# LRU gelu and convolution as side tasks, one weight buffer fewer, and a reordered routing and closing

## The chip, the cores and the metric

One core of one Trainium2 chip runs the whole program. The metric is the device time in microseconds. Before the change three timed runs gave 3310.49, 3309.92 and 3304.97 us, median 3309.92. The profiled execution is a further one, of 3298.6 us.

## The reference, cut to what matters

One layer of a hybrid backbone on 1024 latent tokens and 256 context tokens of width 1024, all in float32.

- An adaLN-modulated RMSNorm of the tokens goes through one input projection. Its columns feed three mixers; of the context, only what the latent scans start from is needed.
- The LRU mixer, which the change touches, has 8 blocks of 128 channels. For each block: a convolution of 4 taps along the tokens (context and latent apart) gives `u`; for each of two directions `r = sigmoid(u @ wa + ba)`, `i = sigmoid(u @ wi + bi)`, `log_a = -8 r softplus(-lambda)`, `v = sqrt(1 - exp(2 log_a)) i u`, and a scan `h = a h + v` that runs through the context and then the latent tokens. The branch is `(h_forward + h_backward) * gelu(y)`, with `y` from another 128 columns of the projection.
- The other two mixers (gated DeltaNet, Mamba-2 SSD) are not touched. The three branches are projected, gated, summed and projected again (`w_out`), and added to the input.
- A second modulated norm feeds a mixture of 32 experts in 4 groups: group logits and expert logits from a router matrix, the best group by its softmax, the two best experts in it by theirs. Each expert computes `(silu(x w1) * (x w3)) w2` on the tokens routed to it, the two results of a token are weighted and added to the residual, and a last RMSNorm gives the output.

## The kernel before, in words

Every large product is split into three fp32r matmuls: an operand is cast to a rounded part (`hi`, ScalarE) and the rest (`lo`, VectorE or GpSimd), and hi·hi, hi·lo and lo·hi are summed in PSUM.

**Phase 1** runs a list of jobs. A job (`run`, L351) takes one block of 128 projection columns: it fetches the split weights (`WBlocks.get`), and multiplies them with the latent tokens (16 groups of 3 matmuls of 512 columns, into one of two PSUM tiles `pj` of 1024 columns), with the context (24 matmuls of 256 columns, into a bank `pjc`), or with both. Then `done` hands the PSUM tile to side tasks. These are generators in a list; between the matmuls of a job `tick` (L392) steps each one that is due. What is due is decided when the program is written out, by a model of the engines' clocks (`Clock`); on the chip each engine then works through its instructions in that fixed order. `live` counts the `pj` tiles that are in use: with two in use the next latent job is not written out before a side task has given one back (`give`). `until(flags)` steps the side tasks, and writes no further job, until the flags are set.

In the LRU stage the jobs of block b are LX+b (latent and context, its values go to the convolution), two jobs of the other mixers that need the context alone, LY+b (latent, its values go to the gelu), and two more such context jobs; four latent jobs for the merge gates follow the last block. `lru_jobs` (L707) makes them. After LX+b, `done` waits with `until` for block b-2 to be written to memory, loads the gate weights `lw` and adds the side task `lru_conv` (L626). That task runs the convolution on one tile `u` of 1280 columns (context and latent), adds one `lru_scan` (L651) for each direction, waits for both, adds their results and multiplies with the gelu. `lru_scan` makes two gates by matmuls on `u` (`psg`, three pieces of up to 512 columns) and a Tanh, and then the decay (`th`, `ea`), the input and the scan; its tiles `tr`, `th` and `ea` have one buffer for each direction, and block b starts its gates when block b-1 has read them for the last time but for `ea` (flag `lt`). After LY+b, `gelu` waits with `until` for block b-1 to be written to memory, since there is one gelu buffer `gl`.

`WBlocks` keeps raw and split weights. The split of the next block goes into the slot that the last job has left. There are two slots for split weights and one for raw ones, and during this stage one more of each (`extra`, in the pool `wx`).

**Out projection and routing.** `out_proj` (L1854) takes eight tiles T of 128 tokens: 48 matmuls each, then `router` of tile T-1 (transposes, logits in `lg`), and `post` of tile T (residual, norm, `h`). After the loop come `route_tokens(0, 7)`, the router of tile 7 and `route_tokens(7, 8)`, which turn logits into experts on VectorE. `route` then counts the tokens of each expert and builds a table of token indices by 16 small matmuls of one-hot matrices `R` and `Bt`.

**Experts.** `experts` (L2256) streams 32 experts: weights are split on ScalarE and VectorE (`wh`, `wl`, three buffers), rows of tokens are gathered, transposed and split (`take`), and the results are scattered to memory (`ys`) by indirect DMAs on GpSimd's queue. `load_x2` loads the residual, two tiles of tokens at a time, on the same queue. After a loop over overflow blocks, `combine` (L2302) loads both results of each token, weights and adds them, and applies the last norm, one tile of 128 tokens after the other.

Of the kernel before, what the change touches and what calls it, by code (L numbers as in the profile page):

```python
# [34 lines left out]
MERGE = (0, 2, 1)  # L35
RAWS = 7
# [232 lines left out]
class Core:  # L269
# [356 lines left out]
    def lru_conv(self, b, ps, wts):  # L626

        lp = self.lp
        u = lp.tile([P, CTX + SEQ], F32, tag="u", name="u")
        cw, cb = self.pp["lcw"][:, 4 * b:4 * b + 4], self.pp["lcb"][:, b:b + 1]  # L630
        yield from self.conv(u[:, CTX:], ps[True], cw, cb, SEQ)
        self.give(ps[True])
        yield from self.wait(("lx", b))
        yield from self.conv(u[:, 0:CTX], ps[False][:, :CTX], cw, cb, CTX)
        self.give(ps[False])
        hs = [None, None]
        for d in range(2):
# [3 lines left out]
        o = u[:, CTX:]  # L641
# [9 lines left out]
    def lru_scan(self, b, d, u, wts, hs):  # L651
# [5 lines left out]
        def gate(w, tag):  # L657
            o = lp.tile([P, n], F32, tag=tag, name="gate", bufs=1)
            i = 4 * b + 2 * d + w
            for n0 in (0, 512, 1024):  # L660
                yield from self.room()
                n1 = min(n, n0 + 512)
                pg = self.aux.tile([P, 512], F32, tag="aux", name="psg")
                nc.tensor.matmul(pg[:, :n1 - n0], lhsT=wts[:, 2 * d + w, :], rhs=u[:, n0:n1], start=True, stop=True)
# [10 lines left out]
        th = lp.tile([P, n], F32, tag=f"th{d}", name="th", bufs=1)  # L675
        ea = lp.tile([P, n], F32, tag=f"ea{d}", name="ea", bufs=1)
# [11 lines left out]
        nc.vector.scalar_tensor_tensor(out=ti, in0=ti, scalar=1.0, in1=u, op0=ALU.add, op1=ALU.mult)  # L688
# [18 lines left out]
    def lru_jobs(self):  # L707
        jobs = []
        for b in range(KT):
            ps = {}  # L710

            def gelu(_, p, lat, b=b, ps=ps):
                if b:
                    self.until(("lre", b - 1))
                ps["ge"] = g = self.lp.tile([P, SEQ], F32, tag="gl", name="gl", bufs=1)
# [4 lines left out]
            def done(_, p, lat, b=b, ps=ps):  # L720
                ps[lat] = p
                if not lat:
                    self.flags.add(("lx", b))
                else:
                    if b > 1:
                        self.until(("lre", b - 2))
                    w = self.lp.tile([P, 4, P], F32, tag="lw", name="lw")
                    self.nc.sync.dma_start(out=w, in_=self.io["lw"][b])
                    self.add(self.lru_conv(b, ps, w))
# [1124 lines left out]
    def out_proj(self, acc):  # L1854
# [20 lines left out]
        def post(T, ps):  # L1875
# [4 lines left out]
            nc.vector.tensor_tensor(out=x2, in0=x2, in1=xt, op=ALU.add)  # L1880
            h = mg.tile([P, D], F32, tag="gt", name="h2", bufs=2)
# [788 lines left out]
```

## Time and profile before

| | us |
|---|---|
| timed runs, median of 3 | 3309.92 |
| profiled execution | 3298.6 |
| its span, first to last instruction | 3296.9 |
| PE busy (89%) | 2918.7 |
| VectorE busy (65%) | 2144.6 |
| ScalarE busy (48%) | 1569.8 |
| GpSimd busy (23%) | 756.0 |
| mean granted TensorE clock | 0.954 of full speed |

PE is the engine that multiplies matrices, DVE is VectorE, ACT is ScalarE, POOL is GpSimd and SP is the engine that issues most DMAs. All times are us from the span's start unless a row says otherwise. A row of a timeline is: start, length, engine, line, operation, tile written <- tiles read, shape, count; in brackets the idle time ahead of it and what ended that. Rows of the same kind that follow each other are merged into one, with a count. Every instruction passes through a helper of the clock model, so all carry the line L255; tiles tell them apart. A matmul of 512 columns whose operands are plain float32, as for `psg`, counts as two.

### The profile page before, as it was taken

The numbers are of one execution on the slowest core, as the hardware profiler recorded it, in microseconds if no ns is written. First come the engines' busy times: TensorE is split into PE (matmuls) and PEld (weight loads), VectorE is DVE, ScalarE is ACT, GpSimd is POOL, SyncE is SP. The second block draws the span as 40 slices with busy tenths as digits, with TensorE's granted clock in tenths as the row PEclk, the third lists the DMA queues.
The fourth block names the chain that finished last, engine by engine and source line by source line (L and its number), as shares of the span: only waits on it lengthen the run. The fifth ranks groups of instructions, "written<-read, shape, count | busy, mean of one in ns | idle before, by whom it ended". The sixth has DMA issues, their size and how long they took to land. (4 is left out here: it accounts for less than half of the span.)

```text
span 3296.9 us, 47286 instructions
## 1 busy us (share of the span) xinstructions
PE 2918.7 (89%) x18539; PEld 2331.5 (71%) x18539; DVE 2144.6 (65%) x3734; ACT 1569.8 (48%) x2260; POOL 756.0 (23%) x638
## 2 busy tenths in 40 slices
PE   7878789989999889899999997979786899999992
PEld 3756667777768667677888886757565788878882
DVE  4676766744744744878888873226635878787785
ACT  4556565344315415455555544111112667677674
POOL 1112121202612621111121111121000233333333
PEclk9989999989999999999999999989898899999996
DMA  5112122211111102021111122455445688898896
GB/s 193 58 58 85 63 76 72 97 40 52 40 38 64 45 26 75 28 52 36 42 37 47 47 78 84 148 216 186 166 158 209 246 331 319 296 342 302 309 351 229
DMA packets 125313, 439.95 MB, mean 133 GB/s; under 512 B 18456, under 2 KB 44312, under 8 KB 99488
## 3 DMA queue, kind: packets, MB, share of 16 engines
q1 hardware_dynamic: 77712, 363.84, 30.7%
q10 hardware_dynamic: 35920, 52.07, 5.2%
q0 software_dynamic: 11456, 21.00, 1.8%
q8 instruction: 147, 2.41, 0.3%
q14 instruction: 78, 0.64, 0.1%
HBM read 393.76 MB, written 64.05 MB: 139 GB/s over the span
## 5 line engine op out<-in xcount | busy, mean ns | idle before, releaser
L255 PE MATMUL pj<-hhi,whi 128*128 128x512 f32 x1616 | 680.4, 422 | 16.9 <-ACT hhi L255 6.8
L255 PE MATMUL pj<-hhi,wlo 128*128 128x512 f32 x1616 | 640.2, 397 | 6.9 <-POOL wlo L255 3.7
L255 PE MATMUL pj<-hlo,whi 128*128 128x512 f32 x1616 | 640.5, 397 | 6.5 <-DVE hlo L255 4.8
L255 DVE TENSOR_TENSOR wl<-raw,wh 128x2048 fp32r<-128x2048 f32 x188 | 448.0, 2403 | 102.7 <-ACT wh L255 100.4
L255 POOL TENSOR_TENSOR wlo<-raw,whi 128x1024 fp32r<-128x1024 f32 x75 | 190.2, 2536 | 1011.4 <-ACT whi L255 939.9
L255 ACT ACTIVATE wh<-raw 128x2048 fp32r<-128x2048 f32 x188 | 360.8, 1919 | 128.2 <-PE psu L255 102.3
L255 PEld LDWEIGHTS pj<-hhi,whi 128*128 128x128 f32 x1616 | 306.1, 190 | 82.6 <-issue 8.4
L255 PEld LDWEIGHTS pj<-hhi,wlo 128*128 128x128 f32 x1616 | 304.8, 189 | 83.3 <-POOL wlo L255 5.3
L255 PEld LDWEIGHTS pj<-hlo,whi 128*128 128x128 f32 x1616 | 306.2, 190 | 72.1 <-DVE hlo L255 7.0
L255 ACT ACTIVATE whi<-raw 128x1024 fp32r<-128x1024 f32 x145 | 152.9, 1057 | 358.1 <-PE pj L255 268.2
L255 PE MATMUL psu<-wl,xh 128*128 128x512 f32 x576 | 227.2, 394 | 3.0 <-DVE wl L255 3.0
L255 PE MATMUL psu<-wh,xh 128*128 128x512 f32 x576 | 227.9, 396 | 0.0
L255 DVE TENSOR_TENSOR wlo<-raw,whi 128x1024 fp32r<-128x1024 f32 x70 | 91.6, 1309 | 208.8 <-ACT whi L255 208.0
L255 PE MATMUL psu<-wh,xl 128*128 128x512 f32 x576 | 226.1, 392 | 0.9 <-DVE xl L255 0.9
L255 ACT ACT_TABLE_LOAD x124 | 159.1, 1283 | 81.2 <-DVE xt L255 32.3
L255 POOL TENSOR_TENSOR yo<-yo,m 128x1024 f32<-128x1024 f32 x35 | 103.6, 2960 | 183.3 <-ACT yo L255 183.2
L255 PE MATMUL psg<-u,lw 128*128 128x512 f32 (+1 forms) x192 | 88.7, 598 | 55.8 <-issue 52.9
L255 PEld LDWEIGHTS psu<-wl,xh 128*128 128x128 f32 x576 | 108.8, 189 | 29.9 <-DVE wl L255 8.4
L255 PEld LDWEIGHTS psu<-wh,xl 128*128 128x128 f32 x576 | 108.7, 189 | 23.6 <-DVE xl L255 1.7
L255 PEld LDWEIGHTS psu<-wh,xh 128*128 128x128 f32 x576 | 109.2, 190 | 22.2 <-ACT xh L255 0.2
L255 PE MATMUL psy<-wh,xh 128*128 128x512 f32 x288 | 117.5, 408 | 0.7 <-ACT xh L255 0.7
L255 PE MATMUL psy<-wh,xl 128*128 128x512 f32 x288 | 114.6, 398 | 0.2 <-DVE xl L255 0.2
(474 smaller groups left out, 5959.2 us busy)
## 6 DMA issues: line engine op xcount, KB each, us to landing
raw<-in_w SPq DMA_DIRECT2D x188, 1024.0 KB
raw<-in_w_in SPq DMA_DIRECT2D x119, 512.0 KB
wr<-in_w_mod ACTq DMA_DIRECT2D x32, 512.0 KB
gate<-gt ACTq DMA_DIRECT2D x48, 256.0 KB
st<-br SPq DMA_DIRECT2D x24, 512.0 KB
raw<-in_w_branch SPq DMA_DIRECT2D x24, 512.0 KB
gt<-gate SPq DMA_DIRECT2D x24, 512.0 KB
wm<-in_w_mod SPq DMA_DIRECT2D x8, 1024.0 KB
```

The source lines that it names most:

```text
L255: return f(*args, **kw)
```

## The change

- `gelu` becomes a side task (`gated`) that keeps its PSUM tile until block b-2 is written to memory and `gl`, now with two buffers, is free. The job list no longer stops there.
- The wait for block b-2 and the load of `lw` move from `done` into `lru_conv`.
- `u` becomes `ul` (latent, 1024 columns) and `uc` (context, 256). The scans are added when the latent part is convolved; the gates take the two latent pieces first and wait for the context part (flag `lc`) before the third. The product with `u` becomes two instructions.
- In `lru_scan` a wait for the sum of block b-1 (flag `lru`) stands ahead of `ea`.
- `WBlocks.extra` no longer adds a third slot for split weights; the second raw slot stays.
- `out_proj`: behind the matmuls of T = 7 come `route_tokens(0, 6)` and the residual of tile 7, then the router of tile 6 and the rest of `post`; at the end the router of tile 7 and `route_tokens(6, 8)`. The Exp of the group logits moves to `route_weights`.
- `route`: `R` and `Bt` are built four at a time by three VectorE instructions with broadcast operands; GpSimd has no part in it.
- `experts`: one weight split instead of two stands ahead of the first tokens; `load_x2` is issued at experts 20, 23, 26 and 29 instead of 29 to 32.
- `combine`: two VectorE instructions add both weighted results to the residual, in place of a ScalarE scaling, a VectorE instruction and a GpSimd addition.

```diff
-    def lru_conv(self, b, ps, wts):
+    def lru_conv(self, b, ps):
         lp = self.lp
-        u = lp.tile([P, CTX + SEQ], F32, tag="u", name="u")
+        if b > 1:
+            yield from self.wait(("lre", b - 2))
+        wts = lp.tile([P, 4, P], F32, tag="lw", name="lw")
+        self.nc.sync.dma_start(out=wts, in_=self.io["lw"][b])
+        ul = lp.tile([P, SEQ], F32, tag="ul", name="ul")
+        uc = lp.tile([P, CTX], F32, tag="uc", name="uc")
-        yield from self.conv(u[:, CTX:], ps[True], cw, cb, SEQ)
+        yield from self.conv(ul, ps[True], cw, cb, SEQ)
         self.give(ps[True])
-        yield from self.wait(("lx", b))
-        yield from self.conv(u[:, 0:CTX], ps[False][:, :CTX], cw, cb, CTX)
-        self.give(ps[False])
         hs = [None, None]
         for d in range(2):
-            self.add(self.lru_scan(b, d, u, wts, hs))
+            self.add(self.lru_scan(b, d, uc, ul, wts, hs))
+        yield from self.wait(("lx", b))
+        yield from self.conv(uc, ps[False][:, :CTX], cw, cb, CTX)
+        self.give(ps[False])
+        yield
+        self.flags.add(("lc", b))
...
-            for n0 in (0, 512, 1024):
+            for n0, n1 in ((CTX, CTX + 512), (CTX + 512, n), (0, CTX)):
+                if not n0:
+                    yield from self.wait(("lc", b))
...
+        if b:
+            yield from self.wait(("lru", b - 1))
         ea = lp.tile([P, n], F32, tag=f"ea{d}", name="ea", bufs=1)
...
             def gelu(_, p, lat, b=b, ps=ps):
-                if b:
-                    self.until(("lre", b - 1))
-                ps["ge"] = g = self.lp.tile([P, SEQ], F32, tag="gl", name="gl", bufs=1)
+                self.add(gated(b, p, ps))
+
+            def gated(b, p, ps):
+                if b > 1:
+                    yield from self.wait(("lre", b - 2))
+                ps["ge"] = g = self.lp.tile([P, SEQ], F32, tag="gl", name="gl")
...
+            if T == 7:
+                self.route_tokens(0, 6)
+                x2 = resid(T, ps)
             if prev:
                 router(*prev)
-            prev = post(T, ps)
-        self.route_tokens(0, 7)
+            prev = post(T, x2 if T == 7 else resid(T, ps))
         router(*prev)
-        self.route_tokens(7, 8)
+        self.route_tokens(6, 8)
...
-        for n in range(16):
...
+        for a in range(0, 16, 4):
+            R = rp.tile([P, 4, P], F32, tag="R", name="R", bufs=2)
+            v.tensor_tensor(out=R, ...is_equal)
+            Bt = rp.tile([P, 4, NC], F32, tag="Bt", name="Bt", bufs=2)
+            v.tensor_tensor(out=Bt, ...is_equal)
+            v.tensor_tensor(out=Bt, in0=Bt, in1=tok..., op=ALU.mult)
...
-        st.split(2)
+        st.split(1)
         x = take(0)
-        st.split(WB - 2)
+        st.split(WB - 1)
...
-            if e > NE - 4:
-                self.load_x2(2 * (e - NE + 3))
+            if e in X2:
+                self.load_x2(2 * X2.index(e))
...
         def weigh(T):
-            nc.scalar.activation(out=y[T][:, 0, :], in_=y[T][:, 0, :], func=AF.Copy, scale=self.wt[:, 0, T:T + 1])
-            nc.vector.scalar_tensor_tensor(out=y[T][:, 0, :], in0=y[T][:, 1, :], scalar=self.wt[:, 1, T:T + 1],
-                                           in1=y[T][:, 0, :], op0=ALU.mult, op1=ALU.add)
+            x2 = self.x2[:, T, :]
+            for k in range(2):
+                nc.vector.scalar_tensor_tensor(out=x2, in0=y[T][:, k, :], scalar=self.wt[:, k, T:T + 1], in1=x2,
+                                               op0=ALU.mult, op1=ALU.add)
         def add(T):
             x2 = self.x2[:, T, :]
-            eng = nc.vector if T == 7 else nc.gpsimd
-            eng.tensor_tensor(out=x2, in0=x2, in1=y[T][:, 0, :], op=ALU.add)
...
-        self.free["w"].append((pool, "x"))
```

## Rows read from the trace of the kernel before

**Rows 1.** Stages: start:end, length, busy (x instructions) by engine, PE clock, DMA share, GB/s.

```profile
95.00:586.00 491.00, 419.61 (x2018) 325.11 (x2017) 331.32 (x388) 280.29 (x352) 89.55 (x38) 0.94 0.21 69
...
2567.00:3238.00 671.00, 656.21 (x3017) 540.79 (x3016) 543.28 (x337) 475.16 (x404) 233.36 (x107) 0.99 0.84 311
```

**Rows 2.** PE's groups in 95 to 600 us: busy, mean ns, idle before.

```profile
L255 PE MATMUL pj<-hhi,wlo 128*128 128x512 f32 x330 | 130.7, 396 | 5.3 <-DVE wlo L255 3.1 <-POOL wlo L255 2.1
...
L255 PE MATMUL psg<-u,lw 128*128 128x512 f32 (+1 forms) x192 | 88.7, 598 | 55.8 <-issue 52.9 <-ACT gate L255 1.7 <-DVE xt L255 1.2
```

**Rows 3.** PE's timeline of the LRU stage, gate matmuls behind long idle times and without.

```profile
177.61 3.99 PE L255 MATMUL psg<-u,lw 128*128 128x512 f32 x6 [6.76 <-issue]
182.15 2.31 PE L255 MATMUL psg<-u,lw 128*128 128x512 f32 x6
...
527.54 4.60 PE L255 MATMUL psg<-u,lw 128*128 128x512 f32 x6 [6.17 <-issue]
```

**Rows 4.** Timelines of VectorE and ScalarE: sum of a block, first decay of the next.

```profile
170.71 1.21 DVE L255 TENSOR_TENSOR u<-ea 128x1024 f32<-128x1024 f32 x1
185.44 1.45 ACT L255 ACTIVATE th<-gate,sp 128x1280 f32<-128x1280 f32 x1
243.58 1.22 DVE L255 TENSOR_TENSOR u<-ea 128x1024 f32<-128x1024 f32 x1
```

**Rows 5.** Weight splits, from the groups of three engines in 95 to 600 us.

```profile
L255 ACT ACTIVATE whi<-raw 128x1024 fp32r<-128x1024 f32 x45 | 47.1, 1053 | 17.2 <-DMA raw<-in_w_in 7.9 <-PE pjc L255 6.1 <-DMA gate<-gt 2.3
...
L255 DVE TENSOR_TENSOR wlo<-raw,whi 128x1024 fp32r<-128x1024 f32 x22 | 31.8, 1444 | 57.9 <-ACT whi L255 57.2 <-PE pjc L255 0.6
...
L255 POOL TENSOR_TENSOR wlo<-raw,whi 128x1024 fp32r<-128x1024 f32 x23 | 62.1, 2699 | 283.9 <-ACT whi L255 247.0 <-DMA tri<-in_masks 20.2 <-DMA raw<-in_w_in 16.6
```

**Rows 6.** PE's timeline: first matmul of three context products, and the one behind them.

```profile
146.38 0.28 PE L255 MATMUL pjc<-chi,whi 128*128 128x256 f32 x1
...
155.01 0.39 PE L255 MATMUL pj<-hhi,whi 128*128 128x512 f32 x1
```

**Rows 7.** Timeline from the last tile of the out projection to the routing.

```profile
2520.31 1.21 DVE L255 TENSOR_TENSOR x<-pj,m 128x1024 f32<-128x1024 f32 x1
...
2527.08 0.17 DVE L255 TENSOR_REDUCE gmx<-lg 128x7 f32<-128x28 f32 x1
...
2535.32 0.19 DVE L255 TENSOR_TENSOR lg<-plt,rb 128x36 f32<-128x36 f32 x1
...
2539.10 0.58 PE L255 MATMUL ptot<-M,um 128*128 128x256 f32 x1 [5.48 <-DVE wt L255]
```

**Rows 8.** VectorE's timeline of the index table.

```profile
2551.63 0.28 DVE L255 TENSOR_SCALAR R<-iota,rk 128x128 f32<-128x128 f32 x1
...
2559.29 0.21 DVE L255 TENSOR_SCALAR hole<-pidx 128x52 f32<-128x52 f32 x1 [1.42 <-PE pidx L255]
...
2561.45 0.67 DVE L255 TENSOR_TENSOR ge<-iota,ob 128x512 f32<-128x512 f32 x1
```

**Rows 9.** PE's timeline: third matmul of the first expert.

```profile
2569.17 0.79 PE L255 MATMUL psu<-wh,xl 128*128 128x512 f32 x1 [0.94 <-DVE xl L255]
```

**Rows 10.** Chain that ended last: the last residual load, and the loads behind it.

```profile
3239.35 6.37 DMA x<-x2d
...
3246.57 0.39 SPq L255
```

**Rows 11.** Scatters of results, 3200 to 3260 us, from issue to landing.

```profile
DMA to landing us min/median/max: 3.3/4.9/10.6
```

**Rows 12.** Timeline of the closing, ScalarE's first instruction and three of VectorE.

```profile
3252.32 1.15 ACT L255 ACTIVATE y<-y,wt 128x1024 f32<-128x1024 f32 x1 [21.39 <-DMA y<-ys]
...
3279.34 1.27 DVE L255 SCALAR_TENSOR_TENSOR y<-y,wt 128x1024 f32<-128x1024 f32 x1
...
3281.21 2.90 DVE L255 SCALAR_TENSOR_TENSOR y<-x,fss,fw 128x1024 f32<-128x1024 f32 x1
...
3291.72 1.29 DVE L255 SCALAR_TENSOR_TENSOR y<-x,fss,fw 128x1024 f32<-128x1024 f32 x1
```

More of the change, by code (lines that the diff above doesn't have):

```diff
@@ L35 @@
 MERGE = (0, 2, 1)
+X2 = (20, 23, 26, 29)
 RAWS = 7
@@ L659, in gate @@
             i = 4 * b + 2 * d + w
[L660 removed]
+            for n0, n1 in ((CTX, CTX + 512), (CTX + 512, n), (0, CTX)):
+                if not n0:
+                    yield from self.wait(("lc", b))
                 yield from self.room()
[L662 removed]
                 pg = self.aux.tile([P, 512], F32, tag="aux", name="psg")
[L664 removed]
+                nc.tensor.matmul(pg[:, :n1 - n0], lhsT=wts[:, 2 * d + w, :], rhs=ul[:, n0 - CTX:n1 - CTX] if n0 else uc, start=True, stop=True)
                 nc.scalar.activation(out=o[:, n0:n1], in_=pg[:, :n1 - n0], func=AF.Tanh, scale=0.5,
@@ L687, in lru_scan @@
         yield
-        nc.vector.scalar_tensor_tensor(out=ti, in0=ti, scalar=1.0, in1=u, op0=ALU.add, op1=ALU.mult)
+        for c, v in ((slice(CTX, n), ul), (slice(0, CTX), uc)):
+            nc.vector.scalar_tensor_tensor(out=ti[:, c], in0=ti[:, c], scalar=1.0, in1=v, op0=ALU.add, op1=ALU.mult)
         yield
@@ L724, in done @@
                 else:
[L725 to L729, printed above, removed]
+                    self.add(self.lru_conv(b, ps))
             jobs += [(LX + b, "both", done), (LY + b, "lat", gelu)]
@@ L1971, in route_tokens @@
         v.tensor_tensor(out=r["gdl"], in0=gl, in1=bc(r["gmx"], 4), op=ALU.subtract)
-        nc.scalar.activation(out=r["gex"], in_=r["gdl"], func=AF.Exp)
+        v.tensor_copy(out=r["gex"], in_=r["gdl"])
         v.tensor_scalar(out=r["gdl"], in0=r["gdl"], scalar1=0.0, scalar2=-8.0, op0=ALU.is_ge, op1=ALU.mult)
@@ L1998, in route_weights @@
         self.nc.scalar.activation(out=wt[:, 1, :], in_=wt[:, 1, :], func=AF.Exp)
-        v.tensor_reduce(out=pg, in_=self.rt["gex"], axis=AX.X, op=ALU.add)
+        gex = self.rt["gex"]
+        self.nc.scalar.activation(out=gex, in_=gex, func=AF.Exp)
+        v.tensor_reduce(out=pg, in_=gex, axis=AX.X, op=ALU.add)
         v.reciprocal(out=pg, in_=pg)
@@ L2078, in route @@
         px = self.aux.tile([P, 512], F32, tag="aux", name="pidx")
-        for n in range(16):
-            R = rp.tile([P, P], F32, tag="R", name="R", bufs=4)
-            v.tensor_scalar(out=R, in0=iot, scalar1=rk[:, n:n + 1], scalar2=None, op0=ALU.is_equal)
-            Bt = rp.tile([P, NC], F32, tag="Bt", name="Bt", bufs=4)
-            eng = nc.gpsimd if n % 2 else v
-            eng.tensor_scalar(out=Bt, in0=iot[:, 0:NC], scalar1=bk[:, n:n + 1],
-                              scalar2=tok[:, n // 8, n % 8:n % 8 + 1], op0=ALU.is_equal, op1=ALU.mult)
-            nc.tensor.matmul(px[:, 0:NC], lhsT=R, rhs=Bt, start=(n == 0), stop=(n == 15))
+        for a in range(0, 16, 4):
+            R = rp.tile([P, 4, P], F32, tag="R", name="R", bufs=2)
+            v.tensor_tensor(out=R, in0=iot.unsqueeze(1).to_broadcast([P, 4, P]),
+                            in1=rk[:, a:a + 4].unsqueeze(2).to_broadcast([P, 4, P]), op=ALU.is_equal)
+            Bt = rp.tile([P, 4, NC], F32, tag="Bt", name="Bt", bufs=2)
+            v.tensor_tensor(out=Bt, in0=iot[:, 0:NC].unsqueeze(1).to_broadcast([P, 4, NC]),
+                            in1=bk[:, a:a + 4].unsqueeze(2).to_broadcast([P, 4, NC]), op=ALU.is_equal)
+            v.tensor_tensor(out=Bt, in0=Bt, in1=tok[:, a // 8, a % 8:a % 8 + 4].unsqueeze(2).to_broadcast([P, 4, NC]),
+                            op=ALU.mult)
+            for i in range(4):
+                n = a + i
+                nc.tensor.matmul(px[:, 0:NC], lhsT=R[:, i, :], rhs=Bt[:, i, :], start=(n == 0), stop=(n == 15))
         dst = t([NC], "dst")
```

8 lines of the change are left out of this document (5 added, 3 removed).

## The prediction

> **What bounds the kernel now.** I read the page first, then the busy time by stage, then for the three stages that the diff touches PE's groups, PE's waits and the timelines of the other engines, and for the end the chain of waits. PE is busy 89% of the span, and in the middle of the experts 98% [rows 1]: nothing gains there unless PE does less, and the change takes no matmul away. The gain must come from where PE stands still: 71.4 us of the LRU stage (491.0 less 419.6) [rows 1], the routing, and the closing, where PE has nothing to do.
>
> In the LRU stage the groups of PE show one cause: of its idle time 52.9 us stand ahead of `psg`, in seven stalls, released by "issue", which is no engine's result but PE's own order [rows 2]. That is how an `until` looks: after LY+b the list stops until block b-1 is in memory, so everything that is due, the gate matmuls of the next block too, is written ahead of the next job, and PE waits there for a `u` that VectorE has not made. The reader should see that the idle time is in front of a side task's matmul and not of a job's. Six of the seven are of this kind (6.8, 8.9, 7.3, 13.7, 7.4 and 6.2, together 50.2; the first and the last stand in [rows 3]). Behind each the clock has fallen: the same six matmuls take 3.9 to 4.6 us where they take 2.31 otherwise [rows 3], six times some 1.9, 11.6 in all. So 61.8 us of PE's time hang on the two `until`.
>
> A second view limits this. The block's sum on VectorE and the first decay of the next block on ScalarE follow each other: 171.9 to 185.4 for the first pair [rows 4], and for the seven pairs of that view 42.8 us together. From decay to sum a block takes 59.4 us [rows 4] (185.4 to 244.8); the eight take 34 to 59, the shortest the last one, which has only gate jobs beside it.
>
> **The change part by part.** All sums are against the profiled execution, 3298.6 us; the median of the timed runs is 11.3 higher, and I put the same difference on it.
>
> *LRU, gelu and convolution as side tasks.* PE goes on with context jobs where it stood. From PE's side that frees up to 61.8 us. From the side of the blocks it frees 42.8 less some 1 us for each pair, 36, if the decays-to-sum stay as long as they are: the new wait ahead of `ea` for the sum of block b-1 keeps blocks one behind the other, as they already are by time. Behind that wait nothing is queued on ScalarE, since a side task that waits writes nothing. What is late next is the PSUM tile: LX+b+1 needs one of two, and they go back when conv(b) and gelu(b) have run, both after block b-2.
>
> *Two slots for split weights instead of three.* This is the price. A context job is 24 matmuls; three in a row with nothing between take 8.63 us, 2.88 each [rows 6]. With two slots the split of the job after next can begin only when the job before has ended, so it has one context job of time. Cast plus rest is 1.05 + 1.44 = 2.5 us if the rest is on VectorE and 1.05 + 2.70 = 3.75 if on GpSimd [rows 5]; they alternate. Each block has four such tight places (the second context job of each pair and the latent job behind it), some 26 in all. Half of them, on GpSimd, are late by 0.9: 12 us. To this comes the queue ahead of the cast and the rest. Its lower bound is 0; as upper bound I take 2 us at each place, 52, since VectorE and ScalarE are busy 67% and 57% of the stage [rows 1] with instructions of 0.3 to 3 us. With three slots PE waits only 5.3 us in the stage for such rests [rows 2], which is nearer to the lower end: I take 0.7, 18 us. Together 30, between 12 and 64.
>
> *Splitting `u`*: 16 products become 32 instructions and two gates wait for `uc` only at their third piece. Some 0.3 us more on VectorE each, 5 us in a stage where it has 160 idle: nothing on the path, at most 5. The load of `lw` stays one DMA per block on SP's queue.
>
> LRU together: 62 - 30 = 32 by PE, 36 by the blocks. I take 33, with ends -5 and 62.
>
> *Out projection and routing.* Before, VectorE runs tile 7's residual and norm from 2520.3 and `route_tokens(0, 7)` from 2527.1 to 2535.3, and only then takes the logits of tile 7 [rows 7], which PE had ready 1.6 us earlier (plt at 2533.6 in PE's timeline). After, six tiles are routed while PE multiplies tile 7: VectorE is free from 2512.3 (end of `h` of tile 6) and needs some 6.4 us: the 8.2 less 1.5 for the Exp and its table, which it now does not wait for, less 0.34 for one tile's maximum. So the residual of tile 7 starts at 2518.7 instead of 2520.3, `h` is done 1.6 earlier, at 2525.6, tile 7's router takes 5.8 without the Exp ahead of it on ScalarE (6.3 with it), and its logits are there at 2531.5. Routing two tiles takes 4.0 (3.8 for one tile, of which 0.3 was the Exp, plus 0.5), so the counting begins at 2535.6 instead of 2539.1 [rows 7]: 3.5 us. The Exp with its table now lies in `route_weights` beside 12 us of index arithmetic on VectorE; without that cover it would cost 1.5.
>
> *Index table.* Before, 7.7 us from the first `R` to the first use [rows 8]. After, four times one instruction of 512 elements (0.67, as `ge` [rows 8]) and two of 208 (0.38 each, as `c` of 224 elements at 2543.0) is 5.7, and the last four matmul pairs at 0.44 each follow, 1.8: 7.5. No change, between -0.5 and +1. The Trainium skill speaks against this edit: "VectorE: DVE Perf Modes", section "Mode 2×_2P — use both read ports for one tensor", has one-source float32 instructions at two elements per cycle and two-source ones at one. By elements alone the edit would then cost an estimated 2.6 us (1232 cycles become 3712, at the page's 0.96 GHz). The rows carry a fixed part that this leaves out: a one-source instruction of 128 elements takes 0.28 us [rows 8], a two-source one of four times as many 0.67.
>
> *First expert.* One split less stands ahead of the tokens' split: 2.2 us of VectorE move behind it. The third matmul waited for that until 2569.2 [rows 9]; now the split follows ScalarE's cast at 2567.0 and 0.65 later PE can go on: 1.1 us, the second split being ready just when PE asks (2572).
>
> *Residual loads.* `load_x2` at experts 20 to 29 costs GpSimd 0.75 us each, on an engine that is busy a third of that stage [rows 1]; PE has no wait on it. At the end it matters: the chain that ended last runs through the last of these loads, issued at 3239.35 behind the last scatter, landing at 3245.7, and SP issues the loads of `y` 0.85 later [rows 10]. Without it they wait for that scatter, issued at 3238.35; scatters land 3.3 to 4.9 us after issue [rows 11]: 3241.7 to 3243.3. Gain 2.5 to 4.1; I take 3.5, as the other megabyte no longer shares the DMA engines.
>
> *Closing.* Before, a tile costs VectorE 1.27 + 0.60 + 2.83: its product, the small steps of the norm with ScalarE's root between, and the last product, which takes 2.90 because GpSimd adds at the same time [rows 12] (1.29 when it does not). 4.7 us a tile. After: 3 x 1.27 + 0.60 = 4.4, and GpSimd is silent. Counted from the first arrival at 3252.3 [rows 12]: eight tiles are 35.3, one table for the root 1.3, end at 3288.9 instead of 3293.0 [rows 12], 4.1 earlier. Bounds: 2 if loads come later than VectorE asks, 5.5 if the steps overlap by 0.1 each.
>
> **Sum.** 33 + 3.5 + 0 + 1.1 + 3.5 + 4.1 = 45.2. Profiled execution 3298.6 - 45.2 = 3253.4; median 3309.9 - 45.2 = 3264.7, so 3265.
>
> **The rivals.** (a) *The wait moves to the PSUM tiles.* PE stops at the next latent job instead of at `psg`, since both tiles wait for block b-2 or VectorE's convolution; the period of a block is that of decay to sum. For it: 59.4 us for block 1 against some 47 of matmuls per block, and blocks without a gap between them (302.6+1.2 to 304.9 in the timelines). It would also be this if the planner set the gates where they stand now. Against it: block 4 took 43 and block 7 34, so the length is not fixed. LRU gives 0 to 15, say 10: 45.2 - 23, median 3288.
>
> (b) *The third weight slot decides, slower.* Place: the 26 tight places. Price: 4 us each instead of 1.15, when the cast stands behind an instruction of ScalarE that itself waits (17.2 us of ScalarE's idle time in front of casts are waits for loads and for PE already [rows 5]). Then 104 us go against 61.8 + 12.2: 30 slower, 3340. It decides from 2.85 us per place. Against it: side tasks fill PE's stalls in the plan, and 5.3 us is all that is lost now.
>
> (c) *Shorter blocks.* With no stall each block also runs faster, and LRU gives over 62: median below 3236.
>
> **How the numbers follow.** Less than 0.2% (6.6 us) is what a measurement of this kernel can't tell from none. Forecast (LRU 15 to 62, median 3236 to 3283): 0.62. Rival (a), 3283 to 3298: 0.22. Rival (c): 0.04. All these are faster: 0.88. Rival (b) holds 0.12: 0.07 where it ends slower by over 6.6, 0.05 within. The range 3238 to 3297 leaves out (b), (c) and the edges of the others, under 0.2.
>
> **What would show it.** In the trace after: no "issue" idle time of 6 us and more ahead of `psg`; matmuls `pj` behind `wlo` with 15 to 50 us of idle time; LRU stage ending near 553 instead of 586. `ptot` 3.5 earlier against the last matmul of the out projection. First load of `y` about 5 us after the last scatter's issue, instead of 8. A tile of the closing in 4.3 to 4.4, with the last product at 1.28. Wrong if PE's idle time ahead of jobs for a PSUM tile (no weights late) is 30 or more, or if waits on `wlo` pass 60.

## The result, and the profile after

The changed kernel takes 3268.05 us (median of 4 runs, 3264.37 to 3272.32), the kernel before 3310.2 (4 runs, 3304.97 to 3310.51): ratio 0.9887, 95% interval 0.9870 to 0.9903, 42 us less. Forecast were 3265 and a gain of 45.2. The execution that was profiled after is the longest of the four, 3272.3 us with a span of 3270.5, so the traces differ by only 26.4 us. From milestones of both (PE's first `pk`, which opens the GDN stage; its last `pw`; the first `bh` product, which opens the merge; the last product of the out projection; the first and the last `psu` of the experts; the end of the span) these come from:

| stretch | before | after | gain |
|---|---|---|---|
| start to end of the LRU stage | 585.5 | 560.7 | 24.8 |
| to the end of the GDN stage | 1428.2 | 1428.8 | -0.6 |
| to the first merge product | 134.8 | 142.8 | -8.0 |
| merge and out projection | 367.1 | 368.1 | -1.0 |
| routing, index table, first gather | 51.4 | 49.9 | 1.5 |
| experts | 656.4 | 656.4 | 0 |
| closing | 73.5 | 63.8 | 9.7 |

The -8.0 stands in code that the change does not touch. The stages of the trace after, in the columns of [rows 1]; the second line is the beginning of that stretch:

```profile
95.00:560.70 465.70, 418.19 (x2006) 326.26 (x2004) 326.37 (x399) 283.53 (x355) 89.48 (x38) 0.97 0.24 74
...
1990.00:2046.00 56.00, 39.49 (x172) 30.98 (x171) 17.91 (x41) 20.92 (x39) 12.83 (x19) 0.76 0.21 66
```

The same stretch in the kernel before, and in a variant of it (E3, below) that leaves this code alone:

```profile
2014.00:2070.00 56.00, 37.72 (x217) 30.12 (x216) 22.79 (x51) 23.08 (x42) 15.46 (x20) 1.00 0.20 67
```

```profile
2015.00:2071.00 56.00, 40.17 (x178) 31.72 (x176) 17.23 (x41) 20.46 (x39) 12.81 (x19) 0.76 0.20 66
```

In two of the three the granted clock is at 0.76 on average over these 56 us, in one at full. Up to the first merge product E3 took 142.2 us, the kernel after 142.8, and E14 143.4 (0.76 too); the ten other variants below, with a clock of 0.88 to 1.00 there, took 134 to 138. The code of this stretch is the same in all of them, so the level does not follow the edits; what sets it is open. Where the change decides I therefore compare stretches of the traces, and use whole times only with their intervals.

**The LRU stage.** TensorE's idle time fell from 71.4 us to 47.5, its busy time stayed (419.6 and 418.2). PE's groups after, as in [rows 2], but with shapes kept apart:

```profile
L256 PE MATMUL pj<-hhi,wlo 128*128 128x512 f32 x357 | 142.4, 399 | 9.2 <-POOL wlo L256 6.5 <-DVE wlo L256 2.8
...
L256 PE MATMUL pjc<-chi,whi 128*128 128x256 f32 x272 | 88.1, 324 | 10.7 <-ACT whi L256 4.7 <-ACT gate L256 4.0 <-ACT se L256 1.8
L256 PE MATMUL pjc<-chi,wlo 128*128 128x256 f32 x272 | 81.1, 298 | 12.8 <-DVE wlo L256 6.7 <-POOL wlo L256 6.1
...
L256 PE MATMUL psg<-ul,lw 128*128 128x512 f32 x128 | 61.8, 597 | 1.6 <-DVE gv L256 0.8 <-PE pj L256 0.5 <-ACT gate L256 0.3
```

and the groups of before that stand against them and were not shown:

```profile
L255 PE MATMUL pjc<-chi,whi 128*128 128x256 f32 x272 | 81.4, 299 | 0.5 <-ACT gate L255 0.4
L255 PE MATMUL pjc<-chi,wlo 128*128 128x256 f32 x272 | 77.3, 284 | 0.0
...
L255 PE MATMUL psg<-u,lw 128*128 128x512 f32 x128 | 72.6, 695 | 52.9 <-issue 52.9
```

Two things are to be seen. The 52.9 us of "issue" ahead of `psg` are gone, and 27.8 us of waits for split weights (`wlo`, `whi`, 17 waits) are there, 5.3 before. And the mean of one matmul has moved: `psg` is faster (695 to 597 ns, 10.8 us in all), `pjc` slower (299 to 324 and 284 to 298; with the third kind, 77.3 to 79.8, that is 13.0 us in all). The low clock has become less (0.97 of full speed over the stage, 0.94 before), and what is left of it has changed its place. PE's timeline after shows how, at the longest of these waits:

```profile
237.68 0.58 PE L256 MATMUL pjc<-chi,wlo 128*128 128x256 f32 x1 [4.85 <-DVE wlo L256]
238.06 0.41 PE L256 MATMUL pjc<-chi,whi 128*128 128x256 f32 x1
...
242.96 0.33 PE L256 MATMUL pjc<-clo,whi 128*128 128x256 f32 x1
243.13 0.28 PE L256 MATMUL pjc<-chi,wlo 128*128 128x256 f32 x1
```

TensorE stood still for 4.85 us, and the job behind that runs at 0.41 us a matmul in place of 0.28: the lower level of the clock (granted clock 0.50 from 237 to 243 us, 1.2 GHz). There are three more such stretches at weight waits (0.50 in 151 to 157, 431 to 434 and 455 to 461 us); behind the rest of the 17 waits the clock stays at full. By the durations of `pjc` in these four, against one such stretch before, some 9 of the 13.0 us are the low clock.

The other view, the chain of the blocks. In the timelines of ScalarE and VectorE after, the decay of block 1 and its sum (as in [rows 4]):

```profile
174.78 1.45 ACT L256 ACTIVATE th<-gate,sp 128x1280 f32<-128x1280 f32 x1
```

```profile
240.44 1.22 DVE L256 TENSOR_TENSOR ul<-ea 128x1024 f32<-128x1024 f32 x1
```

Blocks are counted from 0. From decay to sum this block takes 65.7 us, 58.1 before. Over the eight blocks, from start to start (so a gap holds the 1.2 us of the sum itself):

| | gaps, sum to next decay | decay to sum | last sum | end of stage |
|---|---|---|---|---|
| before | 51.4 | 396.5 | 565.5 | 585.5 |
| after | 8.3 | 425.9 | 550.4 | 560.7 |

The gaps went, 43.1 us, 7 more than the 36 that the prediction had. But the blocks got 29.4 us longer. The chain ends 15.1 us earlier, and the other 9.7 of the 24.8 lie behind it: before, PE still had 20.0 us of jobs to do when the last sum started, and did them without a pause; after, it had 7.4 and waited 3.0 for a load (`kvc`). So the end of the stage is not set by the chain alone.

**Routing to the first expert.** Timelines of PE and VectorE after, as in [rows 7 to 9]:

```profile
2520.83 0.58 PE L256 MATMUL ptot<-M,um 128*128 128x256 f32 x1 [4.37 <-DVE wt L256]
...
2551.33 0.63 PE L256 MATMUL psu<-wh,xl 128*128 128x512 f32 x1
```

```profile
2533.36 0.68 DVE L256 TENSOR_TENSOR R<-iota,rk 128x512 f32<-128x512 f32 x1
...
2536.78 0.69 DVE L256 TENSOR_TENSOR R<-iota,rk 128x512 f32<-128x512 f32 x1 [0.74 <-PE pidx L256]
...
2538.49 0.69 DVE L256 TENSOR_TENSOR R<-iota,rk 128x512 f32<-128x512 f32 x1 [0.32 <-PE pidx L256]
...
2541.91 0.21 DVE L256 TENSOR_SCALAR hole<-pidx 128x52 f32<-128x52 f32 x1 [2.04 <-PE pidx L256]
```

`ptot` comes 3.1 us earlier, counted from the last matmul of the out projection; the table takes 8.55 us, 7.66 before: with two buffers the third and fourth `R` wait for the products of the first two (0.74 and 0.32 us in the rows); the third `psu` has no stall any more.

**Closing.** The chain that ended last, after (as in [rows 10]), and VectorE's timeline (as in [rows 12]):

```profile
3221.67 3.20 DMA ys<-yo,dsti
...
3225.72 6.18 DMA y<-ys
```

```profile
3257.49 1.28 DVE L256 SCALAR_TENSOR_TENSOR y<-x,fss,fw 128x1024 f32<-128x1024 f32 x1
3258.70 2.60 DVE L256 SCALAR_TENSOR_TENSOR x<-y,wt,x 128x1024 f32<-128x1024 f32 x2
...
3261.83 1.28 DVE L256 SCALAR_TENSOR_TENSOR y<-x,fss,fw 128x1024 f32<-128x1024 f32 x1
...
3265.46 1.28 DVE L256 SCALAR_TENSOR_TENSOR y<-x,fss,fw 128x1024 f32<-128x1024 f32 x1
```

The chain now goes from the last scatter straight to the loads of `y`, no residual load between; a tile takes 4.34 us, its last product 1.28.

### The profile page after: what moved, and what is told of

Read it like the earlier page. It is cut to its first block, busy times and chain, and to the rows that moved or that the text cites. A ratio compares the mean times of both kernels' runs of the same rounds, so it can differ in the third digit from the quotient of the medians.

```text
span 3270.5 us, 47231 instructions
## 1 busy us (share of the span) xinstructions
PE 2934.0 (90%) x18539; PEld 2344.0 (72%) x18539; DVE 2141.9 (65%) x3747; ACT 1562.5 (48%) x2252; POOL 729.4 (22%) x623
## 5 line engine op out<-in xcount | busy, mean ns | idle before, releaser
L256 PE MATMUL pj<-hhi,wlo 128*128 128x512 f32 x1616 | 643.7, 399 | 10.8 <-POOL wlo L256 8.1
L256 PEld LDWEIGHTS pj<-hlo,whi 128*128 128x128 f32 x1616 | 307.4, 191 | 73.9 <-issue 7.2
L256 PE MATMUL psy<-wl,xh 128*128 128x512 f32 x288 | 114.8, 399 | 0.0
```

The costliest lines, as they stand in the source:

```text
L256: return f(*args, **kw)
```

## Experiments

Each kernel ran beside the kernel before (medians 3300.6 to 3301.3 in the four sets). The code of the LRU stage after ran unchanged in four profiled kernels, and the stage ended at 560.7, 561.7, 563.4 and 563.7: about 3 us is what this milestone can tell.

**E1 and E2, the change in two halves.** E1 takes the edits of the LRU stage alone (side tasks, two gelu buffers, `uc`, two split slots), E2 routing, experts and closing alone.

> Only the LRU part of the change (gelu and convolution as side tasks, two gelu buffers, context columns apart, no third slot for split weights); routing, experts and closing as before. My theory: the LRU stage ends near 561 us instead of 585.5, PE has no stall ahead of psg and 25 to 32 us of waits for split weights, and what follows is unchanged, so the whole gain is 25 us, 20 to 30 (ratio 0.991 to 0.994). Rival: the 8 us that the changed kernel's trace loses behind the GDN stage at a lower granted clock belong to the LRU change; then this kernel shows the lower clock there too and gains 17 (ratio 0.995).

> Only routing, experts and closing of the change; the LRU part as before. Theory: counting starts 3.1 us earlier, the index table costs 0.9 more, the closing from the last up-projection matmul of the experts to the end is 9.7 shorter: 12 us, 10 to 14 (ratio 0.9955 to 0.997). LRU stage ends at 585 as before. Rival: the closing's gain needs nothing else, but the routing's gain is lost at the first expert: then 10. If this and the LRU part alone add up to less than 30 us, a third thing is in the 42 us between the medians.

E1: 3271.1 us, ratio 0.9916 (0.9888 to 0.9944), stage end 563.4, as its theory had it; the low clock of the rival is not there (0.94 over the 56 us). E2: 3285.8, ratio 0.9954 (0.9938 to 0.9970); its trace has 64.2 us of closing against 73.5, and 48.9 from the out projection to the first `psu` against 51.4: 11.8 us. The two gains add up to 1.3%, the whole change has 1.1 (1.0 to 1.3). Within these intervals the halves do not disturb each other.

**E3, the third split slot alone.** The kernel before without it:

```diff
-        self.free["w"].append((pool, "x"))
```

> The kernel before with the third slot for split weights taken away in the LRU stage and nothing else. Theory A (the price hides behind the stalls): PE waits 25 to 30 us for split weights, but the seven stalls ahead of psg shrink by about as much, since they wait for the block's chain: 0 to 10 us slower. Theory B (the prices add): stalls stay at 50 and the waits for weights come on top: 20 to 30 us slower (ratio 1.006 to 1.009), LRU stage ends at 605 to 615.

3295.8 us, ratio 0.9994 (0.9981 to 1.0007); the stage ends at 583.5, 2.0 earlier than before, which is no difference (E2, with the LRU code of before, ends it at 587.8). PE's waits in it (engine and tile that waits, what it waits for, us in total, times, longest):

```profile
PE psg L255 <- issue: 16.8, 7, 6.7
PE pj L255 <- POOL wlo L255: 9.5, 7, 3.0
PE pj L255 <- DVE wlo L255: 9.2, 5, 3.8
PE pjc L255 <- POOL wlo L255: 7.4, 6, 2.9
PE pjc L255 <- ACT whi L255: 5.9, 5, 2.6
```

With the other two kinds (3.1 and 1.3) 36.4 us of weight waits, 31 more than with the slot, and the "issue" stalls shrink by 36. Theory A: the price I had put at 30 is there on PE, and nothing of it in the time: PE waits for the chain anyway, and which wait it is booked to does not matter.

**E4a, three slots and one gelu buffer.** The room allows no third slot beside two gelu buffers of 32 bits.

```diff
-                if b > 1:
-                    yield from self.wait(("lre", b - 2))
-                ps["ge"] = g = self.lp.tile([P, SEQ], F32, tag="gl", name="gl")
+                if b:
+                    yield from self.wait(("lre", b - 1))
+                ps["ge"] = g = self.lp.tile([P, SEQ], F32, tag="gl", name="gl", bufs=1)
...
+        self.free["w"].append((pool, "x"))
```

> The changed kernel with the third slot for split weights kept and, for the space, one gelu buffer: the gelu side task waits for block b-1, not b-2. Theory A (the weights are what is left): waits for split weights fall from 28 to 5 us, LRU stage ends at 540 to 550 instead of 561, 10 to 20 us faster than the changed kernel. Theory B (the chain of the blocks is what is left): the PSUM tile of the gelu is held longer, PE waits ahead of latent jobs for it instead, and the stage ends at 557 to 570: within 5 us of the changed kernel or slower.

3274.7 us, ratio 0.9926 (0.9900 to 0.9952); the stage ends at 574.7, 14 us after that of the change. In place of the weight waits, of which none is left, PE has

```profile
PE pj L256 <- ACT gl L256: 31.6, 4, 10.7
PE pjc L256 <- ACT gate L256: 8.2, 5, 5.1
```

That is theory B, and rival (a) of the prediction: a latent job waits for its PSUM tile, since gelu, which frees it, waits for its only buffer.

**E4b, E8: two cheap ways at the weight waits.** E4b takes the room for the third slot from the second load slot (`self.free["w"].append((pool, "x"))` in place of the same for `"raw"`). E8 keeps two slots and puts the rest `wlo` of tight places on VectorE, all others of the stage on GpSimd:

```diff
+                    if n < self.end:
+                        eng = nc.vector if n in self.c.tight else nc.gpsimd
```

> The kernel after, with a third slot for split weights as before, bought by giving up one of the two slots into which unsplit weights are loaded (both gelu buffers stay). In the kernel after, TensorE waits 27.8 us in 17 places for split weights in the recurrent-unit (LRU) stage, and its context products (pjc) take 122.8 us together where they took 107.9 before; one such wait of 4.85 us is followed by a granted clock of 0.62 and products of 0.41 us where 0.28 is normal. Theory A (the stage is bound by TensorE; the waits and the low clock behind them are the price of the lost slot): the weight waits fall to some 5 us, pjc falls to about 108, and the stage ends 30 to 37 us earlier than in the kernel after, at 524 to 531. Theory B (with the gaps in the chain of blocks closed, the chain sets the pace): pjc falls as well, but the waits move to products that want a PSUM tile of the chain (pj behind ul or the gelu), 15 us or more, and the stage ends at 550 to 561. Theory C (one load slot is too few): waits for weights stay over 20 us, now behind a DMA, and the stage ends later than 561. I expect B, at about 550, with the whole at 3255 to 3270.

> The kernel after, where in the LRU stage the low part of a job's weights (wlo, the subtraction that ends a split) is put on VectorE (1.2 us when it runs alone) if the job before it is a context job and there is little time, and on GpSimd (2.0 to 3.0) elsewhere; in the kernel after they alternate. Theory A (the price of a place is the duration of the split): the 12.6 us that TensorE waits for GpSimd's wlo shrink by about half, and the stage ends 5 to 9 us earlier. Theory B (the price is set by the queue in front of the split: in the longest wait, 4.85 us, VectorE's wlo stood behind three scans of 5.79 us together, and then shared its time with GpSimd's, 2.67 us for 1.22): the waits behind VectorE's wlo grow by as much as those behind GpSimd's fall, and the stage ends within 3 us of the kernel after, or later. I expect B.

E4b: 3333.7 us, ratio 1.0107 (1.0090 to 1.0124), stage end 637.3; I had expected B; by the stage end it is C, but not by C's mechanism. PE waits 1.9 us for weights; it waits far more for what comes late from ScalarE (26.3 us for the gelu's PSUM tile, 23.6 ahead of `pjc` for a gate). The DMA's wait is ScalarE's, in front of the cast, and everything else on ScalarE is queued behind it:

```profile
ACT whi L256 <- DMA raw<-in_w_in: 80.8, 19, 7.9
```

E8: 3273.0, ratio 0.9918 (0.9901 to 0.9935), stage end 576.3, 15.6 us later: the outcome of theory B, but its mechanism only in part. PE waits 36.3 us for weights, 27.8 after. Ahead of the rest it is 17.2, all VectorE's, where it was 22.1; what grew is the wait for the cast on ScalarE, from 5.7 to 19.1. Why the cast comes later is open. (GpSimd's rest takes 2.34 to 3.43 us in the kernel after, not 2.0 to 3.0 as the expectation has it.)

**E11, the third slot with 16-bit gelu buffers.**

```diff
-                ps["ge"] = g = self.lp.tile([P, SEQ], F32, tag="gl", name="gl")
+                ps["ge"] = g = self.lp.tile([P, SEQ], mybir.dt.bfloat16, tag="gl", name="gl")
...
+        self.free["w"].append((pool, "x"))
```

> The kernel after with the third slot for split weights back, both load slots and both gelu buffers kept; the room for it comes from the gelu buffers, which hold 16-bit values here (bfloat16), so that gelu's result is rounded to 16 bits before the product. Theory A (TensorE sets the pace of the LRU stage of the kernel after; 22.5 us of weight waits and up to 15 us of slower context products behind them are the price of the lost slot): weight waits of 6 us or less, context products at 108 to 111 us in place of 122.8, and the stage ends 25 to 37 us earlier than the 560.7 of the kernel after: 524 to 536. Theory B (the chain of blocks follows right behind and sets the pace): the weight waits go as well, but 15 us or more of waits for the chain's PSUM tiles (pj behind ul or gl) come in their place, and the stage ends at 552 to 562. After the one-gelu variant, where the weight waits went and 31.6 us of waits for gl came, I expect something between, nearer to B: 545 to 556, and the whole 5 to 15 us below the kernel after.

3288.4 us (10 runs), ratio 0.9962 (0.9943 to 0.9980). The weight waits went, and the stage ends at 584.3, 23.6 us later than after. Both theories had it earlier, both fell. PE's waits:

```profile
PE pj L256 <- ACT gl L256: 22.7, 3, 12.4
PE ptr L256 <- ACT xt L256: 12.7, 4, 7.2
PE pk L256 <- DMA kvc<-kvd: 11.0, 1, 11.0
PE pjc L256 <- ACT gate L256: 10.3, 5, 3.9
```

These are scattered over many causes. The chain is not: the sum of block 3 starts at 365.2 in both, that of block 4 at 443.4 against 418.3 (E15's expectation, below, calls these the fifth and the sixth; they are the fourth and the fifth of eight). ScalarE's timeline in block 4:

```profile
375.72 0.47 ACT L256 ACTIVATE gv<-pjc,pp 128x256 f32<-128x256 f32 x1
382.75 1.21 ACT L256 ACTIVATE ul<-pj,pp 128x1024 f32<-128x1024 f32 x1 [6.56 <-DMA br<-ul]
383.85 0.47 ACT L256 ACTIVATE gate<-psg,hb 128x256 f32<-128x256 f32 x1
...
389.50 1.26 ACT L256 ACTIVATE gate<-psg,hb 128x512 f32<-128x512 f32 x2
390.64 1.46 ACT L256 ACTIVATE th<-gate,sp 128x1280 f32<-128x1280 f32 x1
```

The next block's convolution (`ul<-pj`) stands here in front of a piece of the gate of the second direction, and waits 6.56 us for the DMA that still reads its buffer; the decay of that direction comes at 390.6, in the kernel after at 369.8. The condition that the change wrote for the convolution, that block b-2 has been *issued* to memory, lets it be written there. The Trainium skill ("TensorE: Matmul & The Clock Gate", its opening table of facts) calls ScalarE's queue strictly first in, first out; this row agrees, a 0.47 us eviction starting right behind the convolution it has nothing to do with. The same stands in the kernel after in block 5, with a wait of 5.23 us right ahead of the decay of the second direction:

```profile
492.39 1.20 ACT L256 ACTIVATE ul<-pj,pp 128x1024 f32<-128x1024 f32 x1 [5.23 <-DMA br<-ul]
493.49 1.45 ACT L256 ACTIVATE th<-gate,sp 128x1280 f32<-128x1280 f32 x1
```

**E15, E16, E14: the head of ScalarE's queue.** E15 is E11 with one more condition:

```diff
-            yield from self.wait(("lre", b - 2))
+            yield from self.wait(("lre", b - 2), ("lg", b - 1, 1))
```

E16 is the kernel after with the same edit, E14 the kernel after with a third buffer for `ul`; both have the old index table (E5).

> The variant with the third split slot and 16-bit gelu buffers, with one more condition on a block's convolution: it starts only when both decays of the block before have been issued, not as soon as the block two back is written. Its place in the order of ScalarE's work changes, nothing else. In that variant the weight waits were gone, and yet the LRU stage ended at 584.3, 23.6 us after the kernel after; its chain of blocks ran level with that of the kernel after up to the fifth sum (365.2 in both), and the sixth took 78.2 us where the kernel after took 53.1. There ScalarE stood 6.56 us in front of the convolution (ul<-pj), which waited for the DMA that writes the old ul, and the gate tile of the block's second direction was queued behind it: its decay came at 390.6, 369.8 in the kernel after. Theory C (what waits at the head of ScalarE's queue sets the length of a block): the sixth block takes 53 to 60 us, the stage ends at 558 to 568, with no weight waits. Theory A' (some other thing of that variant, its low clock or its waits for gl, makes the stage long): the stage ends within 5 us of 584.

> The kernel after with the old build of the index table (worth 0.8 us in the run of it alone) and with the same condition on the convolution: it starts only when both decays of the block before have been issued. In the kernel after ScalarE waits 9.6 us in three places for the DMA of the old ul (5.2 the longest). Theory C (the head of ScalarE's queue sets the length of a block): the stage ends 3 to 9 us earlier than 560.7. Theory D (the condition takes from the convolution the time in which it stood beside the decays, and the chain gets longer by the conv of a block, some 5 us, in most of the eight blocks): the stage ends 10 us or more later, with waits of TensorE for PSUM tiles (pj behind ul).

> The kernel after with the old build of the index table and with three buffers for the convolution's output ul in place of two (the room is there without the third split slot); the order of issue may shift a little. Theory C: without the wait for the DMA of the old ul (9.6 us in three places of ScalarE's queue) the stage ends 3 to 9 us earlier than 560.7. Theory E (those waits lie beside others and the stage is held by other steps of the chain or by TensorE's own 419 us of work and its weight waits): within 3 us of 560.7, and the whole within 3 us of the variant with the old index table alone (3260.4).

E15: 3242.6 us (3237.2 to 3247.0), ratio 0.9822 (0.9804 to 0.9841), the fastest here, with gelu rounded to 16 bits. E16: 3249.0, ratio 0.9842 (0.9826 to 0.9859), with gelu in 32 bits. E14: 3262.4, ratio 0.9872 (0.9849 to 0.9895), no faster than E5 (below). The LRU stage of E15 and of E16, in the columns of [rows 1]:

```profile
95.00:539.90 444.90, 412.07 (x2011) 321.38 (x2010) 338.57 (x402) 271.29 (x346) 89.74 (x38) 0.98 0.24 75
```

```profile
95.00:550.40 455.40, 418.18 (x2007) 326.34 (x2006) 320.10 (x400) 290.31 (x359) 86.34 (x38) 0.97 0.24 75
```

ScalarE's timeline of E15 where E11 stood:

```profile
364.35 1.46 ACT L256 ACTIVATE th<-gate,sp 128x1280 f32<-128x1280 f32 x1
365.71 1.45 ACT L256 ACTIVATE ea<-gate,sp 128x1280 f32<-128x1280 f32 x1
367.62 1.21 ACT L256 ACTIVATE ul<-pj,pp 128x1024 f32<-128x1024 f32 x1 [0.46 <-DMA br<-ul]
```

The convolution comes behind both decays and finds its buffer all but free. The table of the chain goes on (start to start, us):

| | decay to sum | block 4 | block 5 | last sum | weight waits of PE | end of stage |
|---|---|---|---|---|---|---|
| after | 425.9 | 53.1 | 61.6 | 550.4 | 27.8 | 560.7 |
| E11 | 441.8 | 73.9 | 62.3 | 575.3 | 0 | 584.3 |
| E15 | 396.6 | 52.2 | 52.0 | 529.6 | 0 | 539.9 |
| E16 | 416.1 | 56.0 | 49.6 | 540.4 | 23.4 | 550.4 |
| E14 | 411.0 | 55.7 | 48.7 | 537.7 | 26.6 | 555.5 |

Theory C holds: the edit takes no work away and wins 44.4 us for E11 and 10.3 for the kernel after. Its sizes were off: E15 beat the expected 558 to 568, E16 the 3 to 9. Of the 45.2 us that E15's blocks are shorter than E11's, 38.1 lie in the three blocks in which E11 has the convolution and its wait ahead of the second decay (blocks 4 to 6: waits of 6.56, 6.05 and 2.11 us). The plan orders the other side tasks anew with the edit, so the rest is not assigned.

E14 ends its stage at 555.5, which is C, while the whole is no faster than E5, which is E. By the chain it is no worse than E16: decay to sum 411.0, the last sum 2.7 us earlier. But then PE still has 17.8 us of jobs to do, at full clock and without a pause:

```profile
537.70:555.50 17.80, 17.80 (x78) 14.25 (x77) 6.20 (x3) 3.02 (x5) 4.52 (x2) 1.00 0.53 178
```

With its third buffer the wait for the DMA is gone (9.6 us in three places after), and the order moved too: in block 5 the convolution (481.01) comes behind both decays here as well. So these runs do not tell the DMA's wait and the place of the convolution apart; both edits take the wait from in front of the decay, and block 5 is 12 to 13 us shorter with either.

**E5 and E7, the smaller terms.** E5 is the kernel after with the old build of the index table, E7 with the old closing sums.

> The kernel after with the index table built as before: 16 rounds of one compare (R) on VectorE and one Bt each, alternating with GpSimd, and four buffers, in place of 4 rounds over four tiles at once with two buffers. By the traces, from the first R to the first read of its result it took 7.66 us before and 8.55 after. If that difference is of the build itself (theory A: R of the third and fourth round waits for the products of the first two, as there are two buffers), this kernel shows 7.6 to 7.8 here, and the first expert begins 0.9 us earlier after the last product of the merge stage. If it came from what stands around it (theory B), 8.4 or more stays. A time of the whole can't show it.

> The kernel after with the closing sums as before: ScalarE scales one of the two expert rows, VectorE multiplies and adds the other, and GpSimd (VectorE for the last tile) adds the residual, in place of two multiply-adds on VectorE. From the last expert product to the end it took 73.5 us before and 63.8 after; of these 9.7 I put 4.1 down to the earlier residual loads and 5.5 to the shorter sums. Theory A: this kernel takes 69 to 70 there, its last multiply-adds take 2.5 to 2.9 us each (beside GpSimd's adds) where 1.28 stands after. Theory B (all of it comes from the loads, the sums are hidden between the loads of the tiles): within 1 us of 63.8.

E5's table takes 7.71 us from the first `R` to the first use, theory A; 3260.4 us (2 runs), ratio 0.9882 (0.9862 to 0.9902), not to be told from the change's own. That the two buffers are the cause is read from the waits of the rows; no run has the new build with four buffers. From the out projection to the first `psu` E5 takes 2.5 us less than the kernel after, where 0.9 was expected; but the eight kernels with the new table differ there by 1.5 us among themselves, so the 0.9 is read from the table itself. VectorE in E5:

```profile
2525.86 0.28 DVE L256 TENSOR_SCALAR R<-iota,rk 128x128 f32<-128x128 f32 x1
...
2533.57 0.21 DVE L256 TENSOR_SCALAR hole<-pidx 128x52 f32<-128x52 f32 x1 [1.42 <-PE pidx L256]
```

E7's closing takes 69.8 us (last `psu` at 3196.5, end of span at 3266.3). It lies between 73.5 and 63.8: the earlier loads give 3.7 and the shorter sums 6.0, theory A. VectorE in E7, where the last product of a tile is stretched beside GpSimd's add:

```profile
3240.90 2.90 DVE L256 SCALAR_TENSOR_TENSOR y<-x,fss,fw 128x1024 f32<-128x1024 f32 x1
...
3245.60 2.90 DVE L256 SCALAR_TENSOR_TENSOR y<-x,fss,fw 128x1024 f32<-128x1024 f32 x1
```

A tile every 4.70 us against 4.34 after. From VectorE's first to its last instruction on `y` it takes 39.5 us against 34.8, 4.7 of the 6.0; the rest is that the first tile arrives 0.9 later after the last `psu`, and 0.4 at the end.

## Why the prediction was right, and where it was not

The time was right to 3 us. Neither sign of being wrong came: PE's idle time for a PSUM tile is 2.3 us, not 30, and that behind `wlo` 22.1, not 60. Step by step:

- *The gain is where PE stands still, and the "issue" ahead of `psg` is the cause.* Right: 52.9 us there became 0, and the LRU half has the larger gain (E1 0.8%, E2 0.5%).
- *LRU 33.* The mechanism was right, the size was not: 24.8. The step that failed is "36, if the decays-to-sum stay as long as they are". They went from 396.5 to 425.9, against gaps that gave 43.1. With E15, where they are at 396.6, the gaps give 35.4 and the stage gains 45.6 (the jobs behind the last sum, 9.7 in both, had no term): the condition of that step was the right one, and the change did not meet it. Ten of the 29 us are the convolution ahead of the decays (E16, 416.1; 15 in E14); most of the other 20 go with the third slot (E15 against E16), which also differ by the 16-bit gelu, so that share is not separated.
- *Low clock, 11.6 regained.* `psg` gave back 10.8, but the context products lost 13.0, some 9 of them at the low clock behind weight waits. I had priced those waits by idle time alone.
- *Two split slots, 30.* On PE it is 22.5 of idle time and these 13.0, near what I took; in the time it is -2.0 (E3, no difference) where the chain covers it, and 10.5 (E16 against E15, gelu in 16 bits included) where it does not. Waits of one engine may not be added to a chain that runs on others. Rival (b), the slot making it slower at 4 us a place, did not come: 27.8 us in 17 places are 1.6 each.
- *Rival (a), the PSUM tiles.* One such wait after, 2.3 us (pj behind `ul`). It comes as soon as gelu has one buffer (E4a, 31.6): the second buffer is what kept it away.
- *Routing 3.5.* 3.1 (3.1 to 4.1 in the eleven kernels with this code). *Index table 0, between -0.5 and +1.* 0.9 slower, by two buffers where there were four: I had costed the instructions, and not the wait for a buffer. The elements-only reading of the Trainium skill's "VectorE: DVE Perf Modes" would have had an estimated 2.6; the rows have 0.68 for 512 elements of two sources and 0.28 for 128 of one, as estimated.
- *First expert 1.1.* The stall went, and the first `psu` starts 0.7 later behind the table's first use; from first to last `psu` nothing changed (656.4 both). Counted as a gain, it was none. Part of the 0.7 goes with the new table: that distance is 7.4 in the three kernels that have the old table in the code of after, 7.9 to 8.4 in the eight with the new one. Why is open.
- *Residual loads 3.5, closing 4.1.* 3.7 and 6.0 (E7), of which 4.7 are the steps that I had counted.

Without the 8.0 us of low clock behind the GDN stage the profiled execution would have gained 34.4 where 45.2 stood. That the medians are nearer (42.1) is in part luck. The forecast put the 11.3 us between the profiled and the timed executions of before on the new kernel too; there the median is 4.3 below the profiled one, and these 16 us make a gain of 26 into one of 42. A gain of about 40 is real all the same: E5, the kernel after but for its index table, is 40.2 below the kernel before in the medians and 38.5 in the spans.

## What to carry to other kernels

Before pricing a wait of the busiest engine, ask whether a chain over other engines sets the stage: in E3 31 us of new waits on TensorE cost nothing, and in E11 taking 28 us of them away came with a stage 24 us longer, since the chain's order had changed with it. A side task that may start "when its buffer has been issued to memory" can be written in front of the work that a chain needs, on an engine that runs in order: let it wait for the chain's own instruction instead, which cost one condition here and won 10 to 44 us. Then look at what PE has left to do when the chain ends: E14 shortened the chain as much as E16 and the stage by half of that. A wait of TensorE has a second part behind it, the slower matmuls of the job that follows, and both belong in the price.

## What the runs showed of the hardware

- After 4.85 us without work TensorE took some 5 us at the lower clock (granted clock 0.50, 0.41 us for a context product in place of 0.28), in the middle of a stage whose mean clock is 0.97; four such stretches stand at 17 weight waits, the others left the clock at full.
- The same code, behind the GDN stage, ran with the clock at full in some executions and at 0.76 over 56 us in others: 8 us of a 3270 us kernel, with no edit that it follows.
- A VectorE product of 128x1024 in float32 took 2.90 us beside a GpSimd addition and 1.28 without it (E7 and the kernel after).
